# Two passes over the heads in the second block: k with its Gram blocks first, then q and v with the first solve between them

## The chip, the cores and the metric

The kernel runs on one core of a Trainium2 chip. The metric is the time of one execution on the device in microseconds (us). The engines of a core are TensorE (PE, the matmuls, with its weight loads shown as PEld), VectorE (DVE), ScalarE (ACT), GpSimd (POOL) and SyncE (SP, which here issues the DMAs). A DMA queue is written as SPq.

## The reference, cut to what matters

The program computes two blocks on 1024 tokens of width 1024. The first one (a recurrent branch, a short convolution, a pooling branch) isn't touched. The second prepends 16 meta tokens and runs a mixer and a mixture of experts. The mixer is:

```python
proj = rms_norm_2(h, norm_g) @ w_in
f_in, qkv, z, ab, gate_f, gate_d = jnp.split(proj, points, axis=-1)
fg = f_in.reshape(bsz, seq_len, N_FGROUPS, FGROUP_DIM)            # 4 groups of 128
y_f = real(fft2(fg, axes=(1, 3))).reshape(...) @ w_fourier
qkv = silu(depthwise_conv_centred(qkv, conv_w))                   # 5 taps
q, k, v = jnp.split(qkv, ...)                                     # 8 heads of 128 each
o = gated_delta_chunked(q, k, v, g_f, beta_f) + flip(gated_delta_chunked(flip(q), ...))
y_d = (rms_norm_2(o, out_norm_g) * silu(z)) @ w_delta
merged = sigmoid(gate_f) * y_f + sigmoid(gate_d) * y_d
return merged @ w_out
```

Inside `gated_delta_chunked`, with chunks of 64 tokens:

```python
decay = where(lower, exp(g[:, None] - g[None, :]), 0)
a_mat = where(strict, (k * beta) @ k.T * decay, 0)
t_mat = triangular_solve(eye + a_mat, eye, lower=True, unit_diagonal=True)
qk    = where(lower, q @ k.T * decay, 0)
# then a scan over the chunks with t_mat, qk, k, v
```

So `a_mat` and the solve need k and the gates alone; q is needed for `qk`, v for the scan.

## The kernel before

All heavy products are fp32 split in two parts: `split` gives a high half on ACT (line 170) and the rest on POOL (line 171), and `mm3` (lines 191 to 193) does three matmuls for each k-slice of 128. A weight column of 128 outputs is one `wr` load of 512 KB, one split `wh`/`wl`, and 24 matmuls for each piece of the tokens; `CH2` cuts the 1040 tokens into 348, 346 and 346 columns, `HALF` cuts the 1024 into two of 512.

In the second block the path runs as follows. The gates (`ab`, decays `gc`, `beta`) come first, and `GR` in DRAM holds the cumulative decays as rows. Then one loop over the eight heads: `channels` projects k, q or v of the head, copies the three pieces to `pr` (ACT, line 974), does the first tap on ACT (978), four taps on DVE (980) and the silu on ACT (981). `decays_in` broadcasts the decay rows of the head, `gb`, 576 KB for each of two directions, one buffer each (987). `token_rows` transposes k and q on PE, sums squares on ACT (1010, with its accumulator read) and writes k and q out (`KQs`, `KVs`); `value_rows` does v. `gram_meta` and `gram` subtract decays on DVE (1053, 1067), take the exponential on ACT (1055, 1069), multiply k by [k|q] on PE, 256 columns at once (1078), and form `at` (1083) and `qt` (1085) on DVE; `at` goes to `N2` in DRAM as 128 systems of 64x64 for each direction, `qt` to `QKs`. `table_piece` splits one sixth of the DFT tables for each head.

After the heads comes the Fourier stage: `fourier_in` projects a group, POOL folds it into even and odd parts, PE does two small transforms, POOL forms the sums `fm`, and one `z_gate` (a projection of 2 x 512 columns) stands behind each group, a fifth behind the last. The solves are written ahead of the loop over the groups: `xm`, then for each direction a load of X from `N2`, 62 steps of two DVE operations on a 128x64x64 tile (lines 433 and 435 in the first solve, 417 and 419 in the second), `unit` (a POOL affine_select that clears the other triangle, 424, and a memset of the diagonal, 426), a write of X, and four transposing copies on ACT with a write each (1177, 1178). X and `t` have one buffer each.

The merge with `w_fourier` is 16 units (8 columns of 128, two halves): a gate of 24 matmuls with a sigmoid into a tile `t2` (two buffers), a product of 12 matmuls, one DVE multiplication of 128x512 (1248) and a write to `GF` (1249). PSUM tiles `q` of 512 columns have four buffers (`ps`). Three more z gates and nine units of `gate_d` follow, then the scan.

The order of instructions on each engine isn't that of the text: a scheduler merges the streams, and after that each engine and the SP queue works in its fixed order.

Of the kernel before, what the change touches and what calls it, by code (L numbers as in the profile page):

```python
# [107 lines left out]
NX = 48  # L108

# [21 lines left out]
def body(ctx, tc, A):  # L131
# [281 lines left out]
    def solve_lower(X, n, tmp):  # L413
        for s in range(n - 2, 0, -1):
            m = n - 1 - s
            t = tmp[:, :s * m].rearrange("p (i j) -> p i j", j=s)
            dve.tensor_tensor(t, X[:, s + 1:n, s:s + 1].to_broadcast([X.shape[0], m, s]),
                              X[:, s:s + 1, 0:s].to_broadcast([X.shape[0], m, s]), op=OP.mult)
            dve.tensor_add(X[:, s + 1:n, 0:s], X[:, s + 1:n, 0:s], t)

# [7 lines left out]
    def solve_upper(X, n, tmp):  # L428

        for s in range(1, n - 1):  # L430
            m = n - 1 - s
            t = tmp[:, :s * m].rearrange("p (i j) -> p i j", j=m)
            dve.tensor_tensor(t, X[:, 0:s, s:s + 1].to_broadcast([X.shape[0], s, m]),  # L433
                              X[:, s:s + 1, s + 1:n].to_broadcast([X.shape[0], s, m]), op=OP.mult)
            dve.tensor_add(X[:, 0:s, s + 1:n], X[:, 0:s, s + 1:n], t)  # L435

# [6 lines left out]
    with ExitStack() as ci:  # L443
# [4 lines left out]
        solve_upper(X, 64, t)  # L448
# [431 lines left out]
    KV0 = scratch("KV0", (16, H, 2, P))  # L880
    GR = scratch("GR", (2, 72, P))
# [9 lines left out]
    cq = c2.tile([P, 9, H], F32, name="cq")  # L891
    cw2 = c2.tile([P, 5, 24], F32, name="cw2")
# [7 lines left out]
    pft = sb("ft", 1, cpi, "right")  # L900

    with ExitStack() as cg:
        pg = sb("pg", 1, cg)
        psm = cg.enter_context(tc.tile_pool(name="psm", bufs=2, space=PSUM))
        abT = pg.tile([32, T2], F32, name="abT")
        for c0, n in CH2:
            act.activation(abT[:, c0:c0 + n], q_ab.pop() if q_ab else proj2(w_ab, c0, n, 32), AF.Copy)
        q = psm.tile([P, 9, 32], F32, name="m")
        ab = pg.tile([P, 9, 32], F32, name="ab")
        dve.memset(ab[:, 0], 0.0)  # L910
        pe.transpose(q[:16, 0, :], abT[:, 0:16], ident[:32, :32])
        for i in range(8):
            pe.transpose(q[:, 1 + i, :], abT[:, 16 + i * P:16 + (i + 1) * P], ident[:32, :32])
        dve.tensor_copy(ab[:, 1:], q[:, 1:])
        dve.tensor_copy(ab[:16, 0], q[:16, 0])
        dtb = pg.tile([P, 2, H], F32, name="dtb")
        nea = pg.tile([P, 2, H], F32, name="nea")
        for d_, (dt_, al_) in enumerate(((A.dt_bias_fwd_2, A.a_log_fwd_2), (A.dt_bias_bwd_2, A.a_log_bwd_2))):
            sp.dma_start(dtb[:, d_, :], dt_.broadcast_to([P, H]))
            sp.dma_start(nea[:, d_, :], al_.broadcast_to([P, H]))  # L920
        act.activation(nea, nea, AF.Exp)
        dve.tensor_scalar(nea, nea, -1.0, None, op0=OP.mult)
        abv = ab.rearrange("p c (d b h) -> p d b c h", d=2, b=2)
        sh = [P, 2, 9, H]
        xs, ex, z, z2, g = [pg.tile(sh, F32, name=f"sp{i}") for i in range(5)]
        for d_ in range(2):
            act.activation(beta[:, d_], abv[:, d_, 1], AF.Sigmoid)
            dve.tensor_tensor(xs[:, d_], abv[:, d_, 0], dtb[:, d_:d_ + 1, :].to_broadcast([P, 9, H]), op=OP.add)

        act.activation(ex, xs, AF.Abs)  # L930
        act.activation(ex, ex, AF.Exp, scale=-1.0)
        dve.tensor_scalar(z, ex, 2.0, None, op0=OP.add)
        dve.reciprocal(z, z)
        dve.tensor_mul(z, z, ex)
        dve.tensor_mul(z2, z, z)
        dve.tensor_scalar(g, z2, 1.0 / 15, None, op0=OP.mult)
        for i in (13, 11, 9, 7, 5, 3):
            dve.scalar_tensor_tensor(g, g, 1.0 / i, z2, op0=OP.add, op1=OP.mult)
        dve.scalar_tensor_tensor(g, g, 1.0, z, op0=OP.add, op1=OP.mult)
        dve.tensor_scalar(xs, xs, 0.0, None, op0=OP.max)  # L940
        dve.scalar_tensor_tensor(g, g, 2.0, xs, op0=OP.mult, op1=OP.add)
        for d_ in range(2):
            dve.tensor_tensor(g[:, d_], g[:, d_], nea[:, d_:d_ + 1, :].to_broadcast([P, 9, H]), op=OP.mult)
        dve.tensor_scalar(g[:, :, 0], g[:, :, 0], con2("m16"), None, op0=OP.mult)
        for d_ in range(2):
            q = psm.tile([P, 2, 9, H], F32, name="m")
            pe.matmul(q[:, 0], con2("trif" if d_ == 0 else "trib"), g[:, d_], start=True, stop=True)
            pe.matmul(q[:, 1], con2("ones"), g[:, d_], start=True, stop=True)
            dve.tensor_copy(gc[:, d_], q[:, 0])
            act.activation(dec[:, d_], q[:, 1], AF.Exp)  # L950
            dve.tensor_tensor(ekd[:, d_], q[:, 1], gc[:, d_], op=OP.subtract)
            act.activation(ekd[:, d_], ekd[:, d_], AF.Exp)
            act.activation(eg[:, d_], gc[:, d_], AF.Exp)
            dve.tensor_scalar(neg[:, d_], eg[:, d_], -1.0, None, op0=OP.mult)
            q = psm.tile([72, P], F32, name="m")
            pe.transpose(q, gc[:, d_].rearrange("p c h -> p (c h)"), ident)
            gr = pg.tile([72, P], F32, name="gr", bufs=2)
            dve.tensor_copy(gr, q)
            sp.dma_start(GR[d_], gr)

        KQs_, vs_, sks, gbs = {}, {}, {}, {}

        def channels(h, j, m):

            if j == 0:
                KQs_[h] = pg.tile([P, 2, T2], F32, name="KQ", bufs=2)
            w = w_k if m == 8 else win2.get(512 + m * P)
            pr = pg.tile([P, T2 + 4], F32, name="pr", bufs=2)  # L970
            pool_e.memset(pr[:, 0:2], 0.0)
            pool_e.memset(pr[:, T2 + 2:], 0.0)
            for c0, n in CH2:
                act.activation(pr[:, 2 + c0:2 + c0 + n], q_k.pop() if q_k else proj2(w, c0, n), AF.Copy)
            if j == 2:
                vs_[h] = pg.tile([P, T2], F32, name="v", bufs=2)
            y = KQs_[h][:, j] if j < 2 else vs_[h]
            act.activation(y, pr[:, 0:T2], AF.Copy, scale=cw2[:, 0, m:m + 1])
            for i in range(1, 5):
                dve.scalar_tensor_tensor(y, pr[:, i:i + T2], cw2[:, i, m:m + 1], y, op0=OP.mult, op1=OP.add)  # L980
            act.activation(y, y, AF.Silu)

        def decays_in(h):
            gbs[h] = []
            for d_ in range(2):
                gb = pg.tile([P, 9, P], F32, name=f"gb{d_}")
                sp.dma_start(gb, GR[d_].rearrange("(o c h) t -> o h c t", o=1, h=H)[:, h].broadcast_to([P, 9, P]))
                gbs[h].append(gb)

        def token_rows(h):  # L990

            KQ = KQs_[h]
            ss = pg.tile([P, 2, 9], F32, name="ss", bufs=2)
            dve.memset(ss, 1.0)
            jk = pg.tile([P, P], F32, name="jk")
            for j in range(2):
                if j == 0:
                    q = psm.tile([P, 4, P], F32, name="m")
                    pe.transpose(q[:16, 0, :], KQ[:, 0, 0:16], ident)
                    act.activation(jk[:16], q[:16, 0, :], AF.Square, accum_out=ss[:16, 0, 0:1])  # L1000
                    o = pg.tile([P, 4, P], F32, name="kv", bufs=3)
                    act.activation(o[:16, 0], q[:16, 0], AF.Copy)
                    sp.dma_start(KV0[:, h, 0, :], o[:16, 0])
                for gq in range(2):
                    q = psm.tile([P, 4, P], F32, name="m")
                    for i in range(4):
                        c = 4 * gq + i
                        pe.transpose(q[:, i, :], KQ[:, j, 16 + c * P:16 + (c + 1) * P], ident)
                    for i in range(4):
                        act.activation(jk, q[:, i, :], AF.Square, accum_out=ss[:, j, 1 + 4 * gq + i:2 + 4 * gq + i])  # L1010
                    if j == 0:
                        o = pg.tile([P, 4, P], F32, name="kv", bufs=3)
                        act.activation(o, q, AF.Copy)
                        sp.dma_start(KVs[4 * gq:4 * gq + 4, :, h, 0, :].rearrange("c p n -> p c n"), o)
            for j in range(2):
# [237 lines left out]
    for h in range(5, H):  # L1253
        z_gate(h)
# [861 lines left out]
```

## Time and profile before

| what | us |
|---|---|
| median of three runs (lowest, highest) | 3120.47 (3115.84, 3121.95) |
| profiled execution, its own time | 3117.2 |
| its span | 3115.5 |
| PE busy | 2797.8 (90%) |
| DVE busy | 1516.1 (49%) |
| ACT busy | 1037.2 (33%) |
| POOL busy | 887.3 (28%) |

Busy times are of the whole span; a share of 90% of PE is a mean over stages in which it is full and others in which it isn't. The granted clock of PE is 0.95 of its full speed in the mean. The stages of the second block that the change touches lie between 1229 and 2045 us of the span.

### The profile page before, as it was taken

The page shows a single profiled execution, that of the slowest core. Times are in us where ns is not written, and L with a number is a line of the kernel's source. Part 1 is how long each engine was busy: PE and PEld are TensorE (multiplying, and loading weights), DVE is VectorE, ACT ScalarE, POOL GpSimd, SP SyncE. Part 2 cuts the span into 40 slices and gives each one's busy share as a digit, 9 for nine tenths or more (in the row PEclk, how much of TensorE's full clock was granted, in tenths as well). Part 3 has the DMA queues.
Part 4 walks back from the last instruction along what each step waited for, and adds up shares of the span by engine and source line. Part 5 has one row for each costly group of instructions (what it writes and reads, how often), then busy time and mean ns, then how long its engine had stood idle before and what let it go on. Part 6 is the DMA issues. An engine that isn't in the chain of part 4 may idle for free. (4 is left out here: it accounts for less than half of the span.)

```text
span 3115.5 us, 42978 instructions
## 1 busy us (share of the span) xinstructions
PE 2797.8 (90%) x16109; PEld 2241.1 (72%) x16109; DVE 1516.1 (49%) x2484; ACT 1037.2 (33%) x2049; POOL 887.3 (28%) x705
## 2 busy tenths in 40 slices
PE   7999999999999998789889859999999987878874
PEld 5777777887787876789888747789888763545442
DVE  3344992324412444566668959724564543222316
ACT  4444112222312443565663221234543221111112
POOL 1233233223324442111115922222465300011011
PEclk9999999999999998899999979999999989999996
DMA  4456415444334543455553332399988659999996
GB/s 116 121 147 208 139 43 167 133 141 121 107 111 152 155 144 71 101 148 136 137 141 106 98 132 69 121 267 267 271 243 269 242 218 411 417 404 413 398 362 257
DMA packets 532932, 599.81 MB, mean 193 GB/s; under 512 B 120779, under 2 KB 429183, under 8 KB 512368
## 3 DMA queue, kind: packets, MB, share of 16 engines
q1 hardware_dynamic: 525808, 582.60, 57.8%
q0 software_dynamic: 6912, 14.43, 1.2%
q8 instruction: 128, 2.10, 0.3%
q14 instruction: 84, 0.69, 0.1%
HBM read 473.23 MB, written 134.44 MB: 195 GB/s over the span
## 5 line engine op out<-in xcount | busy, mean ns | idle before, releaser
L171 POOL TENSOR_TENSOR wl<-wr,wh 128x1024 fp32r<-128x1024 f32 x142 | 353.0, 2486 | 733.9 <-ACT wh L170 724.7
L192 PE MATMUL q<-hTh,wl 128*128 128x512 f32 x1040 | 413.1, 397 | 6.8 <-POOL wl L171 6.8
L191 PE MATMUL q<-hTh,wh 128*128 128x512 f32 x1040 | 416.6, 401 | 2.4 <-DVE t L814 1.4
L193 PE MATMUL q<-hTl,wh 128*128 128x512 f32 x1040 | 417.2, 401 | 0.0
L191 PE MATMUL q<-h2h,wh 128*128 128x346 f32 (+4 forms) x1080 | 389.7, 361 | 4.2 <-ACT wh L170 1.6
L192 PE MATMUL q<-h2h,wl 128*128 128x346 f32 (+4 forms) x1080 | 388.1, 359 | 5.6 <-POOL wl L171 5.6
L193 PE MATMUL q<-h2l,wh 128*128 128x346 f32 (+4 forms) x1080 | 385.6, 357 | 0.0
L192 PEld LDWEIGHTS q<-hTh,wl 128*128 128x128 f32 x1040 | 196.9, 189 | 56.6 <-POOL wl L171 8.3
L191 PEld LDWEIGHTS q<-hTh,wh 128*128 128x128 f32 x1040 | 197.0, 189 | 50.3 <-issue 5.8
L193 PEld LDWEIGHTS q<-hTl,wh 128*128 128x128 f32 x1040 | 197.1, 190 | 46.5 <-issue 3.9
L192 PEld LDWEIGHTS q<-h2h,wl 128*128 128x128 f32 (+1 forms) x1080 | 208.8, 193 | 25.5 <-POOL wl L171 7.1
L191 PEld LDWEIGHTS q<-h2h,wh 128*128 128x128 f32 (+1 forms) x1080 | 208.1, 193 | 25.4 <-ACT wh L170 2.1
L193 PEld LDWEIGHTS q<-h2l,wh 128*128 128x128 f32 (+1 forms) x1080 | 208.8, 193 | 18.6 <-issue 0.2
L170 ACT ACTIVATE wh<-wr 128x1024 fp32r<-128x1024 f32 x142 | 148.4, 1046 | 37.5 <-PE q L193 23.1
L433 DVE TENSOR_TENSOR t<-X 128x62 f32<-128x62 f32 (+30 forms) x124 | 150.0, 1210 | 11.8 <-DMA br<-in_w_branch_dram 7.8
L435 DVE TENSOR_TENSOR X<-X,t 128x62 f32<-128x62 f32 (+30 forms) x124 | 148.9, 1201 | 3.5
L1762 POOL DMA_INDIRECT xg<-HN,gidx x28 | 28.7, 1024 | 375.0 <-PE t L1775 303.9
L1781 PE MATMUL q<-mh,xT 128*64 128x256 f32 (+2 forms) x416 | 102.8, 405 | 20.4 <-DMA mh<-in_w_gate_e_dram 20.2
L1781 PE MATMUL q<-yl,xT 128*32 128x256 f32 (+2 forms) x416 | 103.3, 406 | 19.8 <-DMA yl<-in_w_gate_e_dram 19.3
L1783 ACT ACTIVATE sg<-q 128x256 f32<-128x256 f32 x28 | 10.7, 383 | 326.5 <-PE q L1781 326.5
L1784 DVE TENSOR_TENSOR sg<-sg,q 128x256 f32<-128x256 f32 x28 | 11.8, 421 | 204.7 <-ACT sg L1783 204.7
L591 DVE TENSOR_TENSOR t<-t,q 128x512 f32<-128x512 f32 x32 | 21.9, 686 | 172.7 <-PE q L193 164.6
(624 smaller groups left out, 5979.7 us busy)
## 6 DMA issues: line engine op xcount, KB each, us to landing
wr<-in_w_in_dram SPq DMA_DIRECT2D x125, 512.0 KB, 4.5
d<-in_w_down_e_dram SPq DMA_DIRECT2D x38, 1024.0 KB, 18.9
g<-in_w_gate_e_dram SPq DMA_DIRECT2D x25, 1024.0 KB, 9.5
u<-in_w_up_e_dram SPq DMA_DIRECT2D x25, 1024.0 KB, 13.6
KQ<-KQs SPq DMA_DIRECT2D x32, 512.0 KB, 6.8
KV<-KVs SPq DMA_DIRECT2D x32, 512.0 KB, 6.3
wr<-in_w_gate_e_dram SPq DMA_DIRECT2D x26, 512.0 KB, 17.9
mh<-in_w_gate_e_dram SPq DMA_DIRECT2D x13, 1024.0 KB, 12.9
```

The source lines that it names most:

```text
L170: act.activation(hi, src, AF.Copy)
L171: pool_e.tensor_sub(lo, src, hi.bitcast(F32))
L191: pe.matmul(out, sh(k), mh(k), start=(k == 0), stop=False)
L192: pe.matmul(out, sl(k), mh(k), start=False, stop=False)
L193: pe.matmul(out, sh(k), ml(k), start=False, stop=(k == kt - 1))
L433: dve.tensor_tensor(t, X[:, 0:s, s:s + 1].to_broadcast([X.shape[0], s, m]), X[:, s:s + 1, s + 1:n].to_broadcast([X.shape[0], s, m]), op=OP ...
L435: dve.tensor_add(X[:, 0:s, s + 1:n], X[:, 0:s, s + 1:n], t)
L591: dve.tensor_mul(sgm, sgm, q)
L1762: nc.gpsimd.indirect_dma_start(out=xg, out_offset=None, in_=HN, in_offset=bass.IndirectOffsetOnAxis(ap=gi, axis=0), bounds_check=S - 1, oo ...
L1781: up[0] = pe.matmul(qs[r_, j], xT[:, k, r_], w[j][k], start=(k == 0), stop=(k == 7))
L1783: si[0] = act.activation(sg, qs[:, 0], AF.Silu)
L1784: dve.tensor_mul(sg, sg, qs[:, 1])
```

## The change

The loop over the heads becomes a list of slots, one for each piece of a projection. The first eight projections are k's; rows, decays and k blocks of head h are placed three to eight slots behind. The decay tiles after the exponential are written to `DM` in DRAM (four of 256 KB a head). The next sixteen projections are q and v of each head; k and the decays are read back, and `gram_q` multiplies k by q alone. `gb` has two buffers, k three. Three `z_gate`s stand at the end of the slots, four in the Fourier stage, one behind the merge. The first solve is a generator: `start_inverse` loads X, and `advance` lets it do its steps slot by slot until 0.75 of its work is done; the rest is done behind the first two `fourier_in`. Its output and the second solve come after the first Fourier group, the output of the second one behind the fifth merge column. The tables are split at the start of the Fourier stage. The affine_select for X is gone (the memset stays), that of `xm` stays. Square roots for k and q are taken apart.

```diff
+INVSHARE = 0.75
             dve.tensor_add(X[:, 0:s, s + 1:n], X[:, 0:s, s + 1:n], t)
+            yield s * m + 60
...
+    DM = scratch("DM", (2, H, P, 8, P))
...
+    def inverse(d_):
+        X = pi.tile([P, 64, 64], F32, name="X")
+        t = pi.tile([P, 1024], F32, name="t")
+        sp.dma_start(X, N2[d_])
+        xinv[d_] = X
+        yield 0
+        yield from (solve_upper if d_ == 0 else solve_lower)(X, 64, t)
+        dve.memset(X.rearrange("p i j -> p (i j)")[:, 0:64 * 64:65], 1.0)
...
+    def inverse_out(d_):
+        X = xinv[d_]
+        sp.dma_start(TS2[d_], X)
+        for i in range(4):
+            t = pi.tile([P, 16, 64], F32, name="t")
+            act.activation(t, X[:, :, 16 * i:16 * i + 16].rearrange("p s t -> p t s"), AF.Copy)
+            sp.dma_start(TN2[d_, :, 16 * i:16 * i + 16, :], t)
...
-                gb = pg.tile([P, 9, P], F32, name=f"gb{d_}")
+                gb = pg.tile([P, 9, P], F32, name=f"gb{d_}", bufs=2)
...
+        def gram_k(h, gq):
...
+                act.activation(t, t, AF.Exp)
+                sp.dma_start(DM[d_, h, :, 4 * gq:4 * gq + 4, :], t)
...
+                pe.matmul(q[:, i], k[:, tt], k[:, tt], start=True, stop=True)
...
+        def k_back(h):
+            k = ks[h] = pg.tile([P, T2], F32, name="k", bufs=3)
+            sp.dma_start(k[:, 16:].rearrange("p (c t) -> p c t", t=P), KQs[:, :, h, 0, :].rearrange("c p t -> p c t"))
...
+                sp.dma_start(t, DM[d_, h, :, 4 * gq:4 * gq + 4, :])
...
+        def gram_q(h, gq):
...
+                pe.matmul(q[:, i], ks[h][:, tt], qs_[h][:, tt], start=True, stop=True)
...
+                dve.tensor_tensor(qt[d_], q, dms[h, gq][d_], op=OP.mult)
...
+        Q0, Q1 = 3 * H, 9 * H
...
+        at_slot(Q0 + 7, start_inverse)
+        for n in range(Q0 + 11, Q1 + 6):
+            at_slot(n, advance, INVSHARE * (n - Q0 - 10) / (Q1 + 5 - Q0 - 10))
...
+            for h in range(H):
+                yield from channels(8 + h, ks, "k", 3)
+            for h in range(H):
+                yield from channels(h, qs_, "q", 2)
+                yield from channels(16 + h, vs_, "v", 2)
+            for h in range(3):
+                yield from z_gate(h)
...
     fs = [fourier_in(g) for g in range(2)]
...
+    run(inv)
...
-        z_gate(g)
-    z_gate(4)
+        run(z_gate(3 + g))
+        if g == 0:
+            inverse_out(0)
+            run(inverse(1))
...
+            if d == 4:
+                with tc.issue_after(sent.ins), tc.issue_after(gate.ins):
+                    inverse_out(1)
```

The first place is DVE between the last blocks of the heads and the first solve. In the program before, the first solve begins behind the small solve of `xm`, which itself stands behind all heads (433 and 435 are the solve's two operations, X the 128 systems):

```order
L435 TENSOR_TENSOR xm<-xm,t 8x13x2
L433 TENSOR_TENSOR t<-xm 8x14
L435 TENSOR_TENSOR xm<-xm,t 8x14
L433 TENSOR_TENSOR t<-X 128x62
L435 TENSOR_TENSOR X<-X,t 128x62
L433 TENSOR_TENSOR t<-X 128x122
L426 MEMSET xm 8x16
L435 TENSOR_TENSOR X<-X,t 128x2x61
```

In the changed program the same steps (436 and 438) stand in the second pass, between the taps of q and v (1022), the products of q with the decays (1175) and the steps of `xm`:

```order
L1022 SCALAR_TENSOR_TENSOR q<-pr,cw_8901,q 128x1040
L436 TENSOR_TENSOR t<-X 128x950
L1022 SCALAR_TENSOR_TENSOR q<-pr,cw_8901,q 128x1040
L438 TENSOR_TENSOR X<-X,t 128x25x38
L1022 SCALAR_TENSOR_TENSOR q<-pr,cw_8901,q 128x1040
L436 TENSOR_TENSOR t<-X 128x962
L1022 SCALAR_TENSOR_TENSOR q<-pr,cw_8901,q 128x1040
L438 TENSOR_TENSOR X<-X,t 128x26x37
L436 TENSOR_TENSOR t<-X 128x972
L438 TENSOR_TENSOR X<-X,t 128x27x36
```

The solve has moved from behind the last head to among the heads, and the steps now take turns with the convolutions.

The second place is DVE around the merge. Before, the multiplications of the merge (1248, tiles `t`) stand in front of the second solve (417, 419) and then among its steps:

```order
L435 TENSOR_TENSOR X<-X,t 128x62
L426 MEMSET X 128x64
L1248 TENSOR_TENSOR t_14236<-t_14236,q 128x512
L1248 TENSOR_TENSOR t_14332<-t_14332,q 128x512
L1248 TENSOR_TENSOR t_14278<-t_14278,q 128x512
L1248 TENSOR_TENSOR t_14374<-t_14374,q 128x512
L417 TENSOR_TENSOR t<-X 128x62
L419 TENSOR_TENSOR X<-X,t 128x62
L417 TENSOR_TENSOR t<-X 128x122
```

In the changed program the first of them (1341) stand behind the step with 53 rows of the second solve (419, 421):

```order
L419 TENSOR_TENSOR t<-X 128x572
L421 TENSOR_TENSOR X<-X,t 128x52x11
L419 TENSOR_TENSOR t<-X 128x530
L421 TENSOR_TENSOR X<-X,t 128x53x10
L1341 TENSOR_TENSOR t_14646<-t_14646,q 128x512
L1341 TENSOR_TENSOR t_14688<-t_14688,q 128x512
L419 TENSOR_TENSOR t<-X 128x486
L421 TENSOR_TENSOR X<-X,t 128x54x9
L419 TENSOR_TENSOR t<-X 128x440
L1341 TENSOR_TENSOR t_14742<-t_14742,q 128x512
```

Nearly all of the second solve is now ahead of the first multiplication of the merge.

The third place is ACT at the start of the Fourier stage. Before, the four copies t<-X of the first solve (1177) stand among the sigmoids (1244) and splits of the merge:

```order
L170 ACTIVATE fh<-t_14212 128x512
L170 ACTIVATE fh<-t_14216 128x512
L1177 ACTIVATE t<-X 128x1024
L1244 ACTIVATE t_14278<-q 128x512
L170 ACTIVATE wh<-wr 128x1024
L170 ACTIVATE fh<-t_14220 128x512
L1177 ACTIVATE t<-X 128x1024
L1244 ACTIVATE t_14332<-q 128x512
L1177 ACTIVATE t<-X 128x1024
L170 ACTIVATE bh<-br 128x512
L1177 ACTIVATE t<-X 128x1024
L1244 ACTIVATE t_14374<-q 128x512
```

In the changed program they (943) stand among the copies of the Fourier input (1253):

```order
L1253 ACTIVATE f<-q 128x348
L943 ACTIVATE t<-X 128x1024
L1253 ACTIVATE f<-q 128x346 x2
L172 ACTIVATE wh<-wr 128x1024
L943 ACTIVATE t<-X 128x1024
L1253 ACTIVATE f<-q 128x348
L943 ACTIVATE t<-X 128x1024
L1253 ACTIVATE f<-q 128x346
L943 ACTIVATE t<-X 128x1024
L1253 ACTIVATE f<-q 128x346
L172 ACTIVATE wh<-wr 128x1024
```

The copies that wait for the first solve have moved ahead by most of the Fourier stage.

## Rows read from the trace of the kernel before

**Rows 1.** Windows: stretch, length, busy us of each engine (count), clock, DMA share, GB/s.
```profile
1229.00:1645.00 416.00, 360.68 (x2158) 348.06 (x2157) 249.23 (x529) 260.02 (x623) 71.08 (x80) 0.93 0.53 130
1645.00:1802.00 157.00, 141.87 (x737) 122.56 (x735) 145.79 (x118) 45.44 (x86) 116.65 (x90) 0.93 0.31 98
1802.00:1835.00 33.00, 0.40 (x2) 0.38 (x2) 26.02 (x39) 1.40 (x1) 5.74 (x3) 0.56 0.02 8
1835.00:2045.00 210.00, 204.02 (x862) 164.00 (x861) 139.97 (x144) 52.30 (x61) 55.18 (x29) 0.98 0.42 136
```

**Rows 2.** Waits of PE, 1230 to 1645: us in total, times, longest.
```profile
PE m L1008 <- ACT kv L1002: 39.6, 8, 9.9
```

**Rows 3.** Waits of DVE, 1230 to 1645.
```profile
DVE dm L1053 <- DMA NM<-dm: 73.3, 7, 11.2
```

**Rows 4.** Timeline of the SP queue: start, us, instruction, its count.
```profile
1413.07 0.55 SPq L987 DMA_DIRECT2D gb<-GR  x1
```

**Rows 5.** DMA issues, 1230 to 1650: count, KB each, median us to landing.
```profile
gb<-GR SPq DMA_DIRECT2D x16, 576.0 KB, 10.8
```

**Rows 6.** Timeline of DVE: start, us, instruction [idle before, its releaser].
```profile
1273.04 0.22 DVE L1053 SCALAR_TENSOR_TENSOR dm<-gb,gc,C 16x16 f32<-16x16 f32 x1 [10.04 <-DMA gb<-GR]
...
1424.63 0.22 DVE L1053 SCALAR_TENSOR_TENSOR dm<-gb,gc,C 16x16 f32<-16x16 f32 x1 [10.27 <-DMA NM<-dm]
```

**Rows 7.** Waits of PE, 1645 to 2045.
```profile
PE q L193 <- POOL fl L171: 35.7, 2, 32.6
```

**Rows 8.** Timeline of POOL behind the first solve.
```profile
1829.26 4.07 POOL L424 TENSOR_SCALAR_AFFINE_SELECT X<-X 128x4096 f32<-128x4096 f32 x1 [33.78 <-DVE X L435]
```

**Rows 9.** Windows of the instructions on tile X alone.
```profile
1645.00:1802.00 157.00, 0.00 (x0) 0.00 (x0) 139.87 (x86) 0.00 (x0) 0.00 (x0) 0.93 0.31 98
1802.00:1835.00 33.00, 0.00 (x0) 0.00 (x0) 26.02 (x39) 1.40 (x1) 4.07 (x1) 0.56 0.02 8
1835.00:2045.00 210.00, 0.00 (x0) 0.00 (x0) 128.92 (x125) 14.88 (x8) 4.07 (x1) 0.98 0.42 136
```

**Rows 10.** DVE's lines by shape, 1230 to 1645: busy us, mean ns, idle before.
```profile
L980 DVE SCALAR_TENSOR_TENSOR KQ<-pr,cw,KQ 128x1040 f32<-128x1040 f32 x64 | 89.6, 1400 | 30.4 <-ACT KQ L978 29.1
...
L1083 DVE SCALAR_TENSOR_TENSOR at<-g,nbp,dm 128x128 f32<-128x128 f32 x128 | 38.8, 346 | 4.4 <-DMA OFF<-at 2.0 <-ACT dm L1069 2.0 <-DMA wr<-in_w_in_dram 0.3
L1067 DVE SCALAR_TENSOR_TENSOR dm<-gb,gc,C 128x128 f32<-128x128 f32 x128 | 35.1, 346 | 5.0 <-DMA gb<-GR 5.0
```

**Rows 11.** ACT's lines by shape, 1230 to 1645.
```profile
L1010 ACT ACTIVATE jk<-m 128x128 f32<-128x128 f32 x128 | 35.2, 275 | 4.5 <-PE m L1008 1.8
...
L1010 ACT ACTIVATION_READ_ACCUMULATOR jk<-m 128x1 f32 x128 | 25.2, 197 | 0.0
L981 ACT ACT_TABLE_LOAD x17 | 21.8, 1283 | 0.3
...
L978 ACT ACTIVATE KQ<-pr,cw 128x1040 f32<-128x1040 f32 x16 | 18.4, 1150 | 0.0
```

**Rows 12.** Timeline of PE in the merge.
```profile
1799.78 0.40 PE L191 MATMUL q<-fh,bh 128*128 128x512 f32 x1
1800.01 0.39 PE L192 MATMUL q<-fh,bl 128*128 128x512 f32 x1
```

**Rows 13.** DVE's lines by shape, 1645 to 2045.
```profile
L1248 DVE TENSOR_TENSOR t<-t,q 128x512 f32<-128x512 f32 x16 | 10.8, 681 | 22.5 <-ACT t L1244 18.0 <-PE q L193 4.5
```

**Rows 14.** Timeline of DVE in the first and at the second solve.
```profile
1821.75 0.62 DVE L433 TENSOR_TENSOR t<-X 128x440 f32<-128x440 f32 x1
...
1866.66 0.22 DVE L417 TENSOR_TENSOR t<-X 128x62 f32<-128x62 f32 x1 [7.92 <-DMA X<-N]
```

**Rows 15.** Part 5 of the page, the costliest groups.
```profile
L171 POOL TENSOR_TENSOR wl<-wr,wh 128x1024 fp32r<-128x1024 f32 x142 | 353.0, 2486 | 733.9 <-ACT wh L170 724.7
```

**Rows 16.** Timeline of ACT at a table load.
```profile
1376.12 1.28 ACT L1055 ACT_TABLE_LOAD   x1 [8.78 <-DMA NM<-dm]
1377.41 0.21 ACT L1055 ACTIVATE dm<-dm 16x16 f32<-16x16 f32 x1
```

More of the change, by code (lines that the diff above doesn't have):

```diff
@@ L435, in solve_upper, with run @@
             dve.tensor_add(X[:, 0:s, s + 1:n], X[:, 0:s, s + 1:n], t)
+            yield s * m + 60
+    def run(steps):
+        for _ in steps:
+            pass
     GA = scratch("GA", (D, S))
@@ L447, in body @@
         sp.dma_start(X, Ns)
-        solve_upper(X, 64, t)
+        run(solve_upper(X, 64, t))
         unit(X, 64)
@@ L891, in body @@
     cq = c2.tile([P, 9, H], F32, name="cq")
+    sk0 = c2.tile([P, 9, H], F32, name="sk0")
     cw2 = c2.tile([P, 5, 24], F32, name="cw2")
@@ L1129, in body @@
-    FM = scratch("FM", (512, S))
-    GF = scratch("GF", (D, S))
-    GD = scratch("GD", (D, S))
-    Z2 = scratch("Z2", (D, S))
-    OA = scratch("OA", (8, P, H, P))
-    YD = scratch("YD", (D, S))
+    pi = sb("pi2", 1, cpi, "right")
+    cz = ExitStack()
+    pz = sb("pz", 2, cz)
     def half2(w, half):
         return proj2(w, 16 + half * 512, 512)
-    cz = ExitStack()
-    pz = sb("pz", 2, cz)
+    Z2 = scratch("Z2", (D, S))
     def z_gate(h):
@@ L1146, in z_gate @@
             sp.dma_start(Z2[h * P:(h + 1) * P, tt], t)
+            yield
+    def inverse(d_):
[13 more added lines that the diff above has]
+            sp.dma_start(TN2[d_, :, 16 * i:16 * i + 16, :], t)
@@ L1148, in body @@
+    FM = scratch("FM", (512, S))
+    GF = scratch("GF", (D, S))
+    GD = scratch("GD", (D, S))
+    OA = scratch("OA", (8, P, H, P))
+    YD = scratch("YD", (D, S))
+    pft = sb("ft", 1, cpi, "right")
+    tabs = [[pft.tile([KF, 6, NT], F32R, name=f"t{c}{j}") for c in "hl"] for j in range(2)]
     cff = ExitStack()
@@ L1157, in fourier_in @@
         return f
+    for j in range(2):
+        for k in range(0, 6, 2):
+            r = pf.tile([KF, 2, NT], F32, name="raw", bufs=2)
+            sp.dma_start(r, A.dft[j, k * KF:(k + 2) * KF, :].rearrange("(k p) t -> p k t", p=KF))
+            split(r, tabs[j][0][:, k:k + 2, :], tabs[j][1][:, k:k + 2, :])
     fs = [fourier_in(g) for g in range(2)]
-    pi = sb("pi2", 1, cpi, "right")
+    run(inv)
     xm = pi.tile([H, 16, 16], F32, name="xm")
-    tm = pi.tile([P, 1024], F32, name="t")
+    tm = pi.tile([H, 256], F32, name="tm")
     sp.dma_start(xm, NM)
-    solve_upper(xm, 16, tm[:H])
+    run(solve_upper(xm, 16, tm))
     unit(xm, 16)
     sp.dma_start(TM, xm)
-    for d_ in range(2):
-        X = pi.tile([P, 64, 64], F32, name="X")
-        t = pi.tile([P, 1024], F32, name="t")
-        sp.dma_start(X, N2[d_])
-        (solve_upper if d_ == 0 else solve_lower)(X, 64, t)
-        unit(X, 64, d_ == 0)
-        sp.dma_start(TS2[d_], X)
-        for i in range(4):
-            t = pi.tile([P, 16, 64], F32, name="t")
-            act.activation(t, X[:, :, 16 * i:16 * i + 16].rearrange("p s t -> p t s"), AF.Copy)
-            sp.dma_start(TN2[d_, :, 16 * i:16 * i + 16, :], t)
     for g in range(4):
@@ L1243, in body @@
                 sgm = btmp("t2")
-                act.activation(sgm, half2(wg, half), AF.Sigmoid)
+                gate = act.activation(sgm, half2(wg, half), AF.Sigmoid)
                 q = ps.tile([P, 512], F32, name="q")
@@ L1248, in body @@
                 dve.tensor_mul(sgm, sgm, q)
-                sp.dma_start(GF[d * P:(d + 1) * P, tt], sgm)
+                sent = sp.dma_start(GF[d * P:(d + 1) * P, tt], sgm)
+            if d == 4:
+                with tc.issue_after(sent.ins), tc.issue_after(gate.ins):
+                    inverse_out(1)
     cpi.close()
-    for h in range(5, H):
-        z_gate(h)
+    run(z_gate(7))
     QUART = [slice(1, 3), slice(0, 4, 3)]
```

441 lines of the change are left out of this document (233 added, 208 removed).

## The prediction, made before the changed kernel had run

> **What bounds the kernel now.** I read the busy table by stretch first [rows 1]. The change touches only block 2 between 1229 and 2045 us. In these 816 us PE is the fullest engine, but not full: of the 416 us of the q/k/v stage it is busy 361, of the 157 us of the Fourier stage 142, and between 1802 and 1835 it does next to nothing. So the path changes hands, and each place must be read for what ends last there.
>
> In the q/k/v stage PE's largest wait is for ACT's copies, 39.6 us in eight pieces, one per head [rows 2]. ACT is late because DVE is: the wait of DVE at line 1053 sums to 73.3 us in seven [rows 3]. It is put down to a small DMA, but the queue shows what came last: the decay tile `gb` was issued at 1413.07 [rows 4], a `gb` load takes 10.8 us [rows 5], and DVE goes on at 1424.63 [rows 6]. `gb` has one buffer, so each head's load must wait until the head before has used it. The reader is to see a reload in the middle of every head.
>
> The second loss is one block: PE waits 32.6 us for POOL's `fl` [rows 7]. POOL was not busy with it; the affine_select of the solved tile X stood ahead of it in POOL's order, and had waited 33.8 us for DVE's solve [rows 8]. DVE spends 140 + 26 us on the first solve and 129 us on the second [rows 9], and both stand behind all heads. The solve, a chain of small DVE operations, sets the end of the Fourier stage.
>
> **The change, part by part.** I forecast four moments on the old trace's clock: the end of the k work, the start of Fourier (T0), PE's arrival at the third merge product, and DVE's release of it.
>
> *k pass.* The first decays land at 1273 [rows 6]; the gate chain ahead of them is the same arithmetic. From there a head costs DVE 4 taps at 1.40 us, 16 decay subtractions at 0.27 (35.1/128), 16 block products at 0.30 (38.8/128) [rows 10], and some 1.5 us of small operations: 16.4 us. It costs ACT 9 squares at 0.275 + 0.197, four table loads at 1.28 (silu, square root, exp, exp in the new order), and some 5,200 columns of copies, silu and weight half at 1.1 ns (L978: 1040 columns in 1.15 us) plus 0.9 us of small ones [rows 11]: 4.2 + 5.1 + 5.7 + 2.5 for the four exps at the same column price + 0.9 = 18.4 us. Its DMA is two `gb` of 0.58 MB, k rows and columns 1.0, the blocks 0.75, a weight 0.5, and the new write of the decays, 1.0: 4.4 MB. The stage now moves 130 GB/s at a share of 0.53 [rows 1], so 245 GB/s is full, and 4.4 MB are 18.0 us. PE needs 72 matmuls of 346 columns at 0.156 us (512 columns start 0.23 us apart [rows 12], 346 in proportion) and some 2 us more, 13 us. Three resources lie within 2 us of each other; I take 19 us, half a us above the fullest: 1273 + 8 x 19 = 1425. Lower bound 16.4 (-21 us in all); the upper bound is a rival below. `gb` has two buffers here, so its 10.8 us are hidden by the head before; without that cover they would cost what they cost now.
>
> *q and v pass.* The order of the new program puts the first three of these sixteen convolutions ahead of the last k blocks, so DVE has left: 13 convolutions of 5.6 us (73), 32 products of 512 columns at 0.68 [rows 13] (22), the meta solve and small ones (13), and 0.75 of the first solve. What does a solve cost undisturbed? A 440-column step takes 0.62 us, a 62-column one 0.22 [rows 14], a line of 0.155 us + 1.06 ns per column; 124 operations with 83,328 columns give 108 us, so 0.75 is 81. That is 189. The two solves of before took 166 and 129, that is 58 and 21 us more than 108, while POOL was busy 117 of the 157 us and 55 of 210 [rows 1, 9]: 0.5 and 0.4 us per us of POOL. POOL's 16 weight halves at about 2.5 us [rows 15] are 40 us, so another 19. T0 = 1425 + 208, about 1635. PE would have its twelve remaining projections, their transposes and three z gates (48 matmuls of 0.23, 11 us each) done at some 1620, so DVE and PE are near balance; bounds of T0 are 1600 and 1665. Reading k and the decays back (1.5 MB a head, 6 us at 245 GB/s, in 25 us) is hidden by the head's own projections.
>
> The Trainium skill (SBUF — State Buffer, "Who interferes with whom") says that a VectorE operation with two SBUF inputs contends with GpSimd's reads of SBUF. The trace agrees: 166 us for one solve and 129 for the other. What it would do to the second solve is a rival below.
>
> *Fourier to the third merge product.* Before, this is 157 us (1645 to 1802 [rows 1]). One z gate leaves (-11), some 5 us more of merge matmuls lie ahead of the new stop, and the DFT tables are split here now rather than among the heads: +5, an estimate bounded by 0 and by six splits of POOL at 2.5, 15. So PE arrives at 1635 + 156 = 1791.
>
> *Release of that product.* Four PSUM buffers and two `t2` tiles let two units run; the third product needs DVE's first multiplication, which the new order puts behind step 53 of the second solve. DVE's path: a quarter of the first solve, 27 + 3, to 1665; then the hand-over. Before, the last step of solve 1 ended at 1829, where POOL could start [rows 8], and solve 2 began at 1866.7 [rows 14], 37.4 us, of which affine_select's 4.1 is gone: 33, to 1698. Steps 1 to 53 are 99 of the 108 us. POOL is as busy there as in the old Fourier stage (0.74) for the first 95 us, 70 us of POOL at 0.4: 28. Release: 1698 + 127 = 1825. PE waits 34 us, about as long as in the hole that the change removes. A part may come earlier: on ACT the four transposing copies of X stand among the copies of the Fourier input, so these wait for the end of the first solve; that is the same DVE chain, and what PE loses there it doesn't lose again at the product. Bounds: 0 (DVE in time) and 64 (with 0.5 per us and T0 of 1655).
>
> *After it.* Before, 1835 to 2045 is 210 us [rows 1]; z gates 5 and 6 have moved ahead (-22) and the 5 us of matmuls are done: 183. End of this stretch 1825 + 183 = 2008 against 2045, 37 us sooner. What comes behind (scan, experts) is unchanged and takes its inputs with slack: the second hand-over is over at about 1870.
>
> So the gain sits in work moved into idle DVE time, less a new stop that replaces the old one. 3117.2 - 37 = 3080 on the profiled execution, whose time lies 3 us below the median shown (3120.5); I write 3081.
>
> **Rivals.** *DVE in time* (0.20): the spread part of the solve meets little of POOL, T0 is PE's 1620, and the third product is free when PE gets there. Then the end is 1791 + 183 = 1974, 71 us sooner, 3046, and down to 3035 with the earlier T0. For it: PE and DVE are near balance in the second pass. Against: the single buffers of X and `t` keep the two solves and their 33 us in a row.
>
> *The gain is eaten by the second solve* (0.08): it now runs beside the Fourier sums, as the first one did, and pays its excess of 58 us instead of 28; release at 1855, end at 2038, 3110, and with T0 5 us later no change that can be told. The page's rule on the shared port, named above, is what would do this.
>
> *The k pass becomes the bound* (0.17, the slower side): decays, blocks and projections of one head are coupled through one DMA queue, issued in program order. Some 26 issues a head at about 0.55 us [rows 4] hold it 14 us; the new `DM` writes wait for ACT's exp and stand ahead of the next `gb` and weight loads. In the old stage just this coupling made a head 416/8 = 52 us with 31 to 33 us of work on DVE and ACT. Each us per head costs 8: at 19 + 37/8 = 23.6 us a head the gain is gone, at 24.5 it is slower; at 26 the time is 3080 + 56 = 3136. For it: three resources at 16 to 18 us and one order. Against: two `gb` and three k buffers.
>
> *Table loads cost more than their row* (0.03): if an engine switch held ACT twice its 1.28 us, a k head would take ACT 23.5 us and the time would be 3080 + 8 x 4.5 = 3116, no change. The row speaks against it: a load starts at 1376.12 and the next activation at 1377.41 [rows 16]. The Trainium skill (ScalarE: Activation LUTs, "What ACT_TABLE_LOAD costs") gives 1283 ns for the load and some 1380 ns of drain, 2.66 us a switch; the load agrees, the drain is not to be seen in that row.
>
> **How the numbers follow.** The forecast has 0.52. Faster by over 0.2% (6 us, about what a measurement of this kernel can tell from no change) are the forecast, DVE in time, and a small part of the rest: 0.73. The same: most of the two middle rivals, 0.10. Slower: 0.17. The range runs from the first rival (3036) to inside the k-pass rival (3128): below it about 0.07, above it about 0.11. The forecast's own range is 3060 to 3100.
>
> **What would show it.** Right: no DVE wait for `gb` of 10 us per head; no affine_select of 128x4096 on POOL in block 2; projections of q start near 1400 and the Fourier copies near 1635; PE waits once for some 34 us on DVE's line 1341 near 1800, and no hole on `fl`. Wrong: k heads 23 us or more apart with PE waiting for ACT or a DMA; the first solve still running 50 us past T0; or no PE wait on line 1341 at all.

## The result, and the profile after

The changed kernel takes 3152.5 us in the median (3151.7 to 3153.2, four runs) against 3121.2 for the kernel before in the same comparison: ratio 1.0097, interval 1.0071 to 1.0122. It is 1% slower; the forecast was 1.3% faster, and the range ended at 3128. The profiled execution has a span of 3151.5 us, 36.0 more than before. The scan begins 43.5 us later than before (2088.8 against 2045.3), and 7.5 us come back behind its start; so the loss lies between 1229 us and the scan. The end of the stretch is put at 2081 below, which is 2045 moved by the span.

The windows of that stretch, cut some 5 us behind the last k block and behind the last projection, at PE's last matmul before its stop, and at its next (columns as in [rows 1]):

```profile
1229.00:1490.00 261.00, 178.35 (x1056) 172.52 (x1054) 146.40 (x395) 151.91 (x343) 27.75 (x33) 0.83 0.62 154
1490.00:1700.00 210.00, 201.07 (x1245) 192.62 (x1244) 194.45 (x232) 119.93 (x291) 46.19 (x42) 0.98 0.65 190
1700.00:1883.00 183.00, 151.01 (x794) 132.88 (x792) 149.89 (x103) 56.68 (x99) 128.49 (x102) 0.91 0.34 108
1883.00:1917.00 34.00, 0.57 (x2) 0.26 (x2) 32.93 (x34) 0.63 (x1) 2.52 (x2) 0.55 0.00 0
1917.00:2081.00 164.00, 164.00 (x699) 132.53 (x700) 21.77 (x37) 37.59 (x45) 35.03 (x21) 0.99 0.44 136
```

The second row is the stage that the change builds, and it is nearly full: PE 201 and DVE 194 of 210 us. The first row is where the time went. In 261 us PE does 178 us of work, and neither DVE (146) nor ACT (152) is full: three engines wait, and the DMA engines are busy for 0.62 of the time.

Whom PE waits for from 1200 to 2120 us (columns as in [rows 2]):

```profile
PE m L1055 <- ACT kv L1070: 42.5, 5, 13.3
PE q L193 <- DVE t L1341: 32.9, 1, 32.9
PE m L1127 <- ACT kv L1070: 31.7, 4, 11.8
PE m L1293 <- ACT tr L1296: 12.6, 1, 12.6
```

The second row is the stop at the third merge product, foreseen with 34 us. The first and third are the k pass: ACT's copy into `kv` is late. The waits of ACT and then of DVE from 1229 to 1490 say why (columns as in [rows 3]):

```profile
ACT kv L1070 <- DMA KV<-kv: 33.2, 6, 16.1
...
ACT kv L1070 <- DMA KVs<-kv: 13.8, 3, 12.3
```

```profile
DVE dmm L1129 <- DMA NM<-dmm: 48.7, 5, 15.2
DVE dm L1138 <- DMA DM<-dm: 35.6, 4, 16.4
DVE dmm L1129 <- DMA gb<-GR: 12.7, 2, 9.7
```

Nearly all of this waiting is for DMAs of 1 to 256 KB, each of which is small by itself. What they have in common is the SP queue. Its timeline in one k head (columns as in [rows 4], the second number is how long the issue took):

```profile
1335.18 0.46 SPq L1060 DMA_DIRECT2D KQs<-k  x1
1335.69 2.49 SPq L1042 DMA_DIRECT2D gb<-GR  x2
1338.28 7.58 SPq L184 DMA_DIRECT2D wr<-in_w_in_dram  x1
1345.96 7.25 SPq L1133 DMA_DIRECT2D NM<-dmm  x1
1353.31 0.59 SPq L1154 DMA_DIRECT2D N<-at  x1
```

The two decay loads are issued at 1335.69; then the issue of a weight takes 7.58 us instead of half a us, and that of a 1 KB DMA 7.25. From 1335.69 to 1353.31 the queue lets nothing else through, and the next pair is issued at 1368.52: from pair to pair this head takes 33 us and its neighbours 29 to 33, against the 19 that I had. What the DMA engines did meanwhile, in four windows:

```profile
1339.00:1342.00 3.00, 3.00 (x25) 2.96 (x25) 3.00 (x12) 2.62 (x14) 0.00 (x0) 1.00 0.26 64
1342.00:1345.00 3.00, 3.00 (x24) 2.80 (x23) 2.44 (x7) 2.86 (x11) 0.00 (x0) 1.00 0.97 59
1345.00:1348.00 3.00, 3.00 (x21) 3.00 (x20) 0.00 (x0) 2.99 (x5) 0.00 (x0) 1.00 0.65 66
1348.00:1351.00 3.00, 3.00 (x21) 3.00 (x20) 0.00 (x0) 0.83 (x2) 0.00 (x0) 1.00 0.50 86
```

59 to 86 GB/s, a quarter to a third of the 245 GB/s with which I had priced the load, at shares from 0.26 to 0.97. Over the whole 15 us from 1339 to 1354 the mean is 70 GB/s at a share of 0.55: the DMA engines are not full while they move so little. What the loads hold up is seen here (the issues behind them), but not which part of the DMA path they fill.

### The profile page after: what moved, and what is told of

The parts are those of the page before. It is cut to its first block, busy times and chain, and to the rows that moved or that the text cites. A ratio compares the mean times of both kernels' runs of the same rounds, so it can differ in the third digit from the quotient of the medians.

```text
span 3151.5 us, 43378 instructions
## 1 busy us (share of the span) xinstructions
PE 2800.0 (89%) x16237; PEld 2248.9 (71%) x16237; DVE 1506.3 (48%) x2460; ACT 1051.0 (33%) x2065; POOL 879.6 (28%) x703
## 5 line engine op out<-in xcount | busy, mean ns | idle before, releaser
L193 PE MATMUL q<-h2h,wh 128*128 128x346 f32 (+4 forms) x1080 | 391.2, 362 | 38.4 <-DVE t L1341 32.9
L438 DVE TENSOR_TENSOR X<-X,t 128x62 f32<-128x62 f32 (+30 forms) x124 | 135.7, 1094 | 2.3
L436 DVE TENSOR_TENSOR t<-X 128x62 f32<-128x62 f32 (+30 forms) x124 | 125.1, 1009 | 10.7 <-DMA br<-in_w_branch_dram 7.2
L1878 ACT ACTIVATE sg<-q 128x256 f32<-128x256 f32 x28 | 10.8, 384 | 325.7 <-PE q L1876 325.7
L1876 PE MATMUL q<-yl,xT 128*32 128x256 f32 (+2 forms) x416 | 102.8, 405 | 13.3 <-DMA yl<-in_w_gate_e_dram 12.7
```

Source lines behind the costliest of these rows:

```text
L193: pe.matmul(out, sh(k), mh(k), start=(k == 0), stop=False)
L1876: up[0] = pe.matmul(qs[r_, j], xT[:, k, r_], w[j][k], start=(k == 0), stop=(k == 7))
```

## The experiments

Theory Q, formed from these rows: the decay loads hold the DMA side, and with it all issues behind them; the load of nine pieces of 512 B for each partition is slow, whatever buffers wait for it. Rivals: V, the volume of a k head (the new write of the decays); K, two `kv` buffers instead of three. Ratios are to the kernel before on the same chip, with their intervals; code that is left out of an edit is marked by three dots.

**a_row: decays read in one run.** The gates are transposed by head, so that nine rows of a head lie side by side.

```diff
-                pe.transpose(q, gc[:, d_].rearrange("p c h -> p (c h)"), ident)
+                gt = pg.tile([P, H, 9], F32, name="gt", bufs=2)
+                dve.tensor_copy(gt, gc[:, d_].rearrange("p c h -> p h c"))
+                pe.transpose(q, gt.rearrange("p h c -> p (h c)"), ident)
...
-                sp.dma_start(gb, GR[d_].rearrange("(o c h) t -> o h c t", o=1, h=H)[:, h].broadcast_to([P, 9, P]))
+                sp.dma_start(gb.rearrange("p c t -> p (c t)"),
+                             GR[d_, 9 * h:9 * h + 9].rearrange("(o c) t -> o (c t)", o=1).broadcast_to([P, 9 * P]))
```

> The changed kernel with one edit: the rows of the decays stand in DRAM by head, so that a decay tile is read as one run of 4.6 KB for each partition instead of nine of 512 B. The bytes and the number of DMAs stay. Theory Q (mine): the k pass is paced by the SP queue, which the two decay loads of a head block: from their issue to the end of the issues behind them 17.6 us pass of a head of 31 us. Then the issues behind them shorten, a head falls to 18 to 23 us, the last k block is done near 1400 to 1430 instead of 1484, and the time is 3070 to 3105. Theory V (the DMA volume of a head, 4.4 MB with the new write of the decays, paces it): the bytes are the same, so 3145 to 3155. Theory K (two kv buffers instead of three, for which ACT waits): no change, 3145 to 3155.

Measured: 3069.7 us, ratio 0.985 (0.9821 to 0.988). Same bytes, same number of DMAs, and by the two ratios 2.5% or 77 us less than the changed kernel. The DMA view of a_row, 1230 to 1450, answers to [rows 5] and has all sixteen loads; in the changed kernel the row with all sixteen (1229 to 1490) says 14.2, and that of the last eleven (from 1281) 12.5:

```profile
gb<-GR SPq DMA_DIRECT2D x16, 576.0 KB, 5.6
```

And the SP queue of a_row behind the pair of loads:

```profile
1338.21 2.13 SPq L1044 DMA_DIRECT2D gb<-GR  x2
1340.44 0.41 SPq L1144 DMA_DIRECT2D DM<-dm  x1
1340.94 0.46 SPq L184 DMA_DIRECT2D wr<-in_w_in_dram  x1
```

The weight issues in 0.46 us. Its windows there:

```profile
1340.00:1343.00 3.00, 3.00 (x22) 2.88 (x22) 3.00 (x8) 2.88 (x7) 0.00 (x0) 1.00 0.98 241
1343.00:1346.00 3.00, 3.00 (x24) 2.84 (x23) 3.00 (x13) 2.57 (x14) 0.00 (x0) 1.00 0.88 291
```

At shares of 0.98 and 0.88 the DMA engines now move 241 and 291 GB/s. The last k block is done at 1402 instead of 1484; the forecast said 1425. The loads are the cause, with a time at the lower end of what Q expected; V and K fall as the main cause. That it is the SP queue, as Q said when this ran, isn't shown by it: a_gbact asks that.

**b_row: the same edit in the kernel before.**

> The kernel before with the same edit alone. Theory Q, and the prediction's reading that DVE's wait of 10 us per head is the reload of the single decay buffer: the reload falls from 10.8 us to 4 or less, DVE's waits at line 1053 from 73 us to under 30, and the kernel gains 30 to 50 us, 3070 to 3090. If the wait belongs to another DMA or the cost is in the bytes: no change, 3115 to 3125.

Measured: 3063.1 us, 0.9825 (0.9801 to 0.985): 53 us, a little more than expected. DVE's wait at the line of [rows 3] (1056 here) falls from 73.3 to 31.8 us, and a load lands in 5.2 us instead of 10.8 (1230 to 1650). So the reading of the old profile (the wait is the reload of `gb`) was right, and what it cost could be won back without a second pass. Against b_row, the two passes with the same repair (a_row) gain nothing.

**a_gb1: the second decay buffer taken away again** (`bufs=2` to `bufs=1` for `gb`).

> The changed kernel with one decay buffer for each direction instead of two, as the kernel before had it. The prediction hides the decay load behind the head before, thanks to the second buffer. If the load could be hidden at all: without the second buffer a head grows by some 10 us, 3210 to 3240. If the loads hold the DMA engines and the queue whenever they are issued, the second buffer gives little: 3145 to 3180.

Measured: 3146.0 us, 1.0101 (1.0078 to 1.0125); the changed kernel has 1.0097. With the loads as they are, the buffer that was to hide them is worth nothing that can be told. Now DVE waits openly for the load, in the waits of 1229 to 1490:

```profile
DVE dmm L1129 <- DMA gb<-GR: 63.3, 8, 10.1
DVE dm L1138 <- DMA gb<-GR: 37.0, 7, 6.5
```

100 us, against 97 in the three rows shown for the changed kernel. With two buffers about as much time is waited under other names, behind the load in the queue.

**a_gbact: the loads in a queue of their own** (`sp.dma_start(gb, ...)` becomes `act.dma_start(gb, ...)`).

> The changed kernel with one word changed: the decay loads are issued by ACT instead of SP, so that they stand in a queue of their own; their nine pieces of 512 B per partition stay. Theory Q1 (it is the SP queue, in its order, that the loads block): SP's other issues take 0.4 to 0.6 us again, a k head falls from 31 to 20 to 25 us, and the time is 3080 to 3115. Theory Q2 (the small pieces hold the DMA engines, from whichever queue they come): the k pass stays within 20 us of what it is, 3125 to 3150.

Measured: 3136.9 us, 1.0061 (1.0041 to 1.0082), some 11 us less than the changed kernel; the last k block is done at 1467. So it is hardly the order of the SP queue: the loads hold up other DMAs from either queue (Q2). An issue of SP beside a load still takes up to 9.3 us here. The 11 us are net, since ACT now pays the issues of the loads (up to 4.9 us for one). The Trainium skill (DMA: Bandwidth & Descriptors, "Issuing engines are not separate DMA queues") says that DMAs started by different engines run on the same 16 DMA engines and interleave there, so that another issuer saves only its issue time. The run agrees, with 11 of 77 us.

**a_nodm: no write of the decays.**

```diff
-                sp.dma_start(DM[d_, h, :, 4 * gq:4 * gq + 4, :], t)
...
-                sp.dma_start(t, DM[d_, h, :, 4 * gq:4 * gq + 4, :])
+                sp.dma_start(t, KQs[4 * gq:4 * gq + 4, :, h, 0, :].rearrange("c p t -> p c t"))
```

> The changed kernel without the write of the decays to DRAM (32 DMAs of 256 KB); the q pass reads columns of k in their place, the same bytes, so the products of q are not those of the reference. Theory Q: only four short issues of 0.4 to 0.5 us a head go, 3135 to 3152. Theory V: a quarter of the volume of a k head goes, 4 us or more a head, 3100 to 3125. Theory K: no change.

Measured: 3125.5 us, 1.0029 (1.0016 to 1.0043), 0.7% or 21 us under the changed kernel, between the two expectations, at the edge of V's: a smaller gain than V needs as the main cause, and a larger one than Q allowed. The writes cost 0.7 us for each of the 32 of 256 KB, together a quarter of what a_row gains.

**a_kv3: three `kv` buffers** (`gr` has one instead of two).

> The changed kernel with three kv buffers as before (the small gr tile has one instead of two, to make room). ACT waits 47 us in the k pass for the DMAs out of kv. Theory K: most of that goes, 3100 to 3125. Theory Q: the DMAs stand late in the queue, so a third buffer only lets ACT wait elsewhere, 3140 to 3155. Theory V: the same as Q.

Measured: 3141.0 us, 1.0076 (1.005 to 1.0103), some 7 us less than the changed kernel, which the intervals can't tell from nothing. ACT's waits for the two DMAs out of `kv` all but go (6.4 us left of 47), and PE then waits 65.5 us for DVE where it had waited 74 for ACT: the wait moves elsewhere, as Q says.

The rest asks what the other parts of the change are worth once the loads are repaired.

**a_row_s0 and a_row_end: the first solve not spread.** The first sets `INVSHARE` to 0. Its trace shows the steps of the solve from 1427 to 1645, among the projections all the same: the program's order of instructions puts them where DVE has room, and the share decides little. The second ties them down; `last_qt` is the last product of q with the decays:

```diff
-INVSHARE = 0.75
+INVSHARE = 0.0
...
-    run(inv)
+    with tc.issue_after(last_qt[0].ins):
+        run(inv)
```

> The version a_row with no share of the first solve among the projections (0 instead of 0.75), so that all of it stands behind the first Fourier inputs. If the DVE chain sets the end of the Fourier stage, as the prediction says: the q and v pass is up to 10 us shorter, but the first solve ends some 130 us later against it, the four copies of X on ACT hold the Fourier inputs until then, and the time is 3160 to 3210. Rival: the q and v pass is so full that the spread only moves DVE's work about, then within 30 us of a_row, 3050 to 3100.

> The version a_row with the first solve tied behind the last product of q with the decays, so that none of its steps can stand among the projections (in a_row_s0 the order of instructions kept them there). If the DVE chain sets the end of the Fourier stage: the q and v pass may end up to 10 us sooner, the first solve ends 110 to 140 us later against it, the copies of X hold the Fourier inputs, and the time is 3150 to 3200. Rival (the spread only moves DVE's work about): within 30 us of a_row, 3045 to 3100.

Measured: 3071.7 us (0.9851, 0.9832 to 0.9871) and 3064.6 us (0.9832, 0.9816 to 0.9849). Now the first solve runs from 1588 to 1756 and the second begins 110 us later than in a_row, and the time is about the same. My expectation failed. The waits of PE in a_row_end:

```profile
PE q L193 <- ACT ch L172: 31.7, 1, 31.7
PE q L193 <- ACT bh L172: 11.4, 1, 11.4
PE q L194 <- POOL cl L173: 10.1, 4, 5.8
...
PE q L193 <- DVE t L1347: 8.4, 1, 8.4
```

In a_row the largest is 30.5 us for DVE at the third merge product. The stage of the projections without the solve (a_row_end, columns as in [rows 1]):

```profile
1400.00:1600.00 200.00, 195.00 (x1235) 187.23 (x1234) 119.01 (x155) 124.02 (x308) 39.05 (x41) 0.99 0.69 205
```

PE is as full as before and DVE is not: 119 of 200 us. From the last k block to the first Fourier matmul it is 205 us (1399 to 1604), against 212 in a_row (1402 to 1614). So PE sets the length of this stage, and the spread adds some 7 us to it.

Without the spread, ACT's copy of X stands in front of a split of the Fourier stage and waits 33.5 us for the first solve; the merge multiplications then stand early in the second solve. There is one stop of some 30 us in either, only in another place.

**b_row_na: the affine_select taken away alone** (from b_row, the memset stays).

> The version b_row (the kernel before with the decays read in one run) without the affine_select of the two large X, as in the change; the memset of the diagonal stays. If the stop of 33 us on fl is POOL's order, as the prediction says: it goes, and the next stop is DVE's order at the hand-over or nothing; 3030 to 3045. Rival: the stop moves to the wait of the transposing copies or to the merge's multiplication behind the second solve, 3055 to 3065.

Measured: 3063.0 us, 0.9818 (0.9795 to 0.984), the same as b_row, as the rival had it. The 34.8 us for `fl` go, and this row of PE's waits has taken their place:

```profile
PE q L191 <- ACT fh L170: 32.7, 2, 31.5
```

The transposing copy of X stands ahead of the next `fh` on ACT, and waits for the same solve.

**a_row_sp2 and a_sp2: the second solve handed out behind the merge multiplications**, with and without the repaired loads.

```diff
-            run(inverse(1))
+            steps, spent[0] = [inverse(1)], 0
+            next(steps[0])
+        advance(0.15 * g)
...
-                dve.tensor_mul(sgm, sgm, q)
+                prod = dve.tensor_mul(sgm, sgm, q)
...
+                with tc.issue_after(prod.ins):
+                    advance(0.45 + 0.06 * (2 * d + half + 1))
             if d == 4:
+                run(steps.pop() if steps else ())
```

> The version a_row with the second solve handed out as well: by steps behind each Fourier group and each multiplication of the merge, so that the first multiplication stands behind step 29 instead of step 53. If the stop of 30 us at the third merge product is only DVE's order: it goes, 3035 to 3050. Rival: the end of the solve, now later, holds the scan instead, 3060 to 3075.

> The changed kernel with the second solve handed out behind the multiplications of the merge, the decays read in nine pieces as in the change. If the two losses are apart from each other: the stop of 33 us at the third merge product goes and the k pass stays as it is, 3110 to 3125, no longer slower than before. Rival (PE's time in the Fourier stage is set by the late k pass anyway): 3140 to 3155.

Measured: 3035.0 us, 0.9732 (0.9711 to 0.9752), and 3110.8 us, 0.9978 (0.9968 to 0.9987). The stop of DVE's order goes in both, 1.2% or 37 us by the ratios; PE's largest wait left in a_row_sp2 is 12.7 us. The two losses are apart from each other, and a_row_sp2 is the fastest version, 2.7% under the kernel before.

**b_row_sp: one pass, with the loads in one run, no affine_select, and both solves handed out.** 44 steps of the first solve stay ahead of the merge; the rest, the copies and the second solve stand behind its multiplications by `issue_after`.

> One pass over the heads as before, with the decays read in one run, without the affine_select of the two large X, and with both solves handed out behind the multiplications of the merge and their copies behind the splits. If the two passes are what makes room for the solves: the second solve ends too late for the scan here, 3050 to 3065. If the order around the merge is all that is needed: the stop of 33 us goes, 3025 to 3040, as fast as two passes with the same two edits (3035).

Measured: 3052.8 us, 0.9795 (0.9779 to 0.9812). The stop at the merge is gone, but a part comes back at the scan:

```profile
PE v L1355 <- DMA KV<-KV: 22.9, 1, 22.9
```

That fits the first expectation: with one pass the solves end late for the scan. The second solve ends at 1956 us, the last of its copies is sent at 1976.5, and the loads for the scan stand behind it in the queue (1978.2). That no other order would do better isn't settled by this one.

## Why the prediction was wrong

Its moments, on each kernel's own clock (k end: end of line 1151's last group; release: first multiplication at line 1341; lines 1154 and 1344 in a_row):

| moment | forecast | changed kernel | a_row |
|---|---|---|---|
| end of the last k block | 1425 | 1484 | 1402 |
| start of the second solve | 1698 | 1758.7 | 1677 |
| PE's stop at the third merge product | 34 | 32.9 | 30.5 |
| release of that product | 1825 | 1916.2 | 1834 |
| end of the stretch (2045 before, moved by the span) | 2008 | 2081 | 1999 |

**The step that failed is the price of a k head's DMA.** I divided 4.4 MB by 245 GB/s, 18.0 us, and took 19 us for a head; and I let the second buffer hide the 10.8 us of a decay load. The rows of before spoke against both: 576 KB in 10.8 us [rows 5] are 55 GB/s, not 245, and two of these one behind the other are 21.6 us a head, more than any term that I had (18.4 at most). Taking an average rate for a transfer that had a row of its own was the error. Before, the two loads of a head lay 20 to 29 us apart in a head of 48; in a k head there is nothing to put between them. A pair took some 15 us at 70 GB/s (1339 to 1354); with the other 3.2 MB at 245 GB/s, 13 us, that gives 28 us, an estimate from these two figures, and from the first decays at 1261 to the last block at 1484, the eight heads took 28 us each. The pass began 12 us sooner than the 1273 that I had read off, and ended 59 us late. a_row shows this term alone: with the load at 5.6 us the heads take 18.6 us each (1253 to 1402), close to my 19, and the kernel 3070, 11 us under the forecast. That the time lies so near is in part luck: in a_row the pass begins 20 us sooner than I had it, and the second solve takes 30 us longer.

It was the third rival (0.17, at 26 us a head 3136) that came about, with its direction and place; its mechanism, the order of one queue, is by a_gbact only a small part (11 of 77 us). I gave it too little, and the range ended inside it. The sign that the prediction named for it came: k heads over 23 us apart, with PE waiting for ACT.

**The other terms.** The sum was -37 and became +36: +59 in the k pass, +2 up to the start of the second solve, +30 in its first 53 steps (157 us instead of 127), and -18 behind the release (165 instead of 183, counted to 2081; to the scan itself it is 173, and the rest comes back behind its start). There PE is busy without a gap, where it had idled for 6 of 210 us before [rows 1].

The second solve is the second rival, right in mechanism and size. Its two lines from 1700 to 1960:

```profile
L421 DVE TENSOR_TENSOR X<-X,t 128x62 f32<-128x62 f32 (+30 forms) x62 | 89.8, 1449 | 2.1
L419 DVE TENSOR_TENSOR t<-X 128x62 f32<-128x62 f32 (+30 forms) x62 | 73.8, 1191 | 31.7 <-DMA X<-N 29.7
```

163.6 us, where it had 129 in its old place [rows 9] and 108 undisturbed (the prediction's estimate). Its first 53 steps took 157 us, 58 more than the 99 undisturbed, as that rival had it. The forecast counted 70 us of POOL at 0.4; POOL was busy for 104 of the 157 us (1759 to 1916), which makes 0.56 us for each us of POOL. A step of one size, with POOL at work and with POOL idle:

```profile
1773.73 7.62 DVE L421 TENSOR_TENSOR X<-X,t 128x572 f32<-128x572 f32 x1
...
1914.03 0.75 DVE L421 TENSOR_TENSOR X<-X,t 128x572 f32<-128x572 f32 x1
```

From 1773.04 to 1780.73 POOL ran seven operations without a pause, and from 1887 to 1925 none: the excess lies where POOL works. The Trainium skill's rule (SBUF — State Buffer, "Who interferes with whom") is that a VectorE operation with two SBUF inputs contends with GpSimd's reads of SBUF. The trace agrees, with 7.62 us against 0.75, though it doesn't show the port itself. The idle 29.7 us of the row of line 419 is the hand-over of X, forecast at 33.

The q and v pass came out as forecast, 210 us, but that is in part luck. I had it from DVE's work, 208 us, with PE done after 195. In a_row_end DVE has far less to do there, and the pass still takes 205 us: PE's work was some 10 us longer than I had it, and happened to lie near DVE's sum. The stop that takes the old one's place was right to 1 us. But what it is worth was read wrongly: the spread of the first solve was to pay for it, and a_row_end shows that the spread pays nothing in this order of instructions. Nor did table loads matter: with them a head took 18.6 us in a_row, where that rival (0.03) needed 23.5 on ACT alone. A slip of the last sum, 3081 for 3080 + 3, changes nothing here.

## What to carry to other kernels

Price a transfer by its own row, not by the mean rate of the stage: a load that moves 55 GB/s where the stage moves 130 is the first thing to mend. A second buffer didn't hide it here (a_gb1), because other DMAs that the engines needed were held up behind the load. Where one solve or chain feeds three engines, taking a stop off one of them moves it to the next (fl, fh, ch, the multiplication: some 30 us each time); what helped is to put the chain's later steps behind the work that others wait for. Test the small part of a large change first: here one edit of the layout gave 53 us, the rebuilt loop nothing beside it until the second solve was handed out as well.

## What the runs showed of the hardware

A broadcast of nine 512 B rows to 128 partitions (576 KB) took 10.8 us to land in the kernel before and 14.2 in the changed one, where a pair of them ran at 59 to 86 GB/s with a mean DMA share of 0.55; as one run of 4.6 KB a partition it took 5.2 us in b_row and 5.6 in a_row. Why the nine pieces are slow stays open: the edit makes one piece out of nine, and it also brings rows together in DRAM that lay 4 KB apart; the 128 readers of the same rows are there with both. A single issue behind such loads took 6 to 9 us instead of 0.4 to 0.6. A DVE step of two inputs in SBUF took 7.62 us beside a POOL at work and 0.75 us without. The stalls also cost PE its clock: in the head shown the granted clock is 1.00 (2.4 GHz) up to 1357 and 0.50 (1.2 GHz) from 1360 to 1367, after PE had had nothing to do since 1352; the mean is 0.83 from 1229 to 1490 and 0.98 in the full pass behind it.
